# A two-layer float32 kernel on one core: wide and narrow products of a weight tile paired one by one, with a re-laid second norm and modulation products spread earlier

## The chip, the cores and the metric

The kernel runs on one core of one Trainium2 chip. The metric is the device time of one execution in microseconds; the kernel before has a median of 2358.75 us over 3 runs (2356.71 to 2363.08). Its profiled execution took 2357.4 us, of which the trace's span is 2355.7 us. Engine names: PE is the matrix engine (PEld its weight loads), DVE the vector engine, ACT the scalar engine, POOL the general engine, SP the engine that issues most loads.

## The reference

Two blocks follow each other on 256 tokens of width 2048, all in float32. What matters here of the first block:

```
mod = silu(c) @ w_mod + b_mod; sh1, sc1, g1, sh2, sc2, g2 = split(mod, 6)
hx  = rms_norm(x, norm1_g) * (1 + sc1) + sh1
z   = hx @ w_in                       # q, gates, v, g, sb, sc, sh, ga, gb
o   = scan over tokens, both directions, started from the states that ctx leaves
y_a = norm(o) * silu(g);  y_b = sb * short_conv(sc * sh)
x   = x + g1 * ((sigmoid(ga) * (y_a @ w_pa) + sigmoid(gb) * (y_b @ w_pb)) @ w_o)
h   = rms_norm(x, norm2_g) * (1 + sc2) + sh2
a, b = split(h @ w_up, 2);  a = conv 3x3 on a 4 x 64 grid of tokens (a) + bias
x   = x + g2 * ((silu(a) * b) @ w_down)   # 5632 channels
return rms_norm(x, final_g)
```

The second block norms its input with 16 added rows, forms q, k, v and gates by products with `w_in_2`, runs two kinds of attention (one with normed and rotated q and k: `qk_norm`, `diff`; one of a stick-breaking kind: `stick`), and returns the input plus the gated result times `w_out_2`.

## The kernel before

Every large product is done in three float32r parts: each operand is split into a high part and a low rest, and high x high, high x low and low x high are summed in PSUM. Weights come from memory in tiles of 128 x 1024 elements (512 KB), loaded by `blocks`: one load into `raw` on SP's queue, then ACT makes `whi` (L156), then DVE makes `wlo` = raw - whi (L157). There are four buffers each of `raw`, `whi` and `wlo`; 680 tiles go through in all. The two conversions are given a high priority in the ordering of instructions; all other vector work is ordered behind or between them by a list scheduler that sets one fixed order for each engine.

Three forms of product use these tiles. `gemm_tf` (L239 to L241) has the weights as the moving operand, 512 columns each. `gemm_ft` has them as the stationary operand with two sources. `gemm_wide` also has them as the stationary operand: for each 128 x 128 piece of `whi` a product with 512 moving columns (high and low part of the activations beside each other), here called wide, and for each piece of `wlo` a product with 256 columns (the high part alone), here called narrow. Both go through `mat` (L296). A tile holds eight pieces; in the kernel before all eight wide products of a tile come first, then all eight narrow ones. `gemm_wide` is called 32 times (2 in the recurrent stage, 22 in the feed-forward stage, 8 in the second block), 8 tiles each: 256 tiles, 2048 pairs of a wide and a narrow product.

The stages follow each other in time: first norm (0 to 205 us), recurrent (to 430), rest of the mixer (to 1024, its last product is with `w_o`), feed-forward (to 1785; four, four and three steps of `up`, each group followed by `down`), second block (to the end). Work that isn't a large product is written as generators in a list `bg`; `pump`, called after each weight tile, advances them by a step or more. A separate generator, `late_mod`, forms the modulation values that are needed from `w_o` on: in 128 steps it loads 512 KB of `w_mod` on POOL's queue (L663) and multiplies and adds them on DVE (two instructions a step, L697 and L700, of 128 x 512 each). `late_rate` (0.42) is the number of such steps for each pump. Where a value is needed and isn't there yet, the code pumps until it is (`while self.n_mod < 9 + n`).

At the end of the mixer, `add_rows` adds the gated product to x (L1103, L1104), `squares` sums squares on ACT, `rsqrt_mean` makes the factor `r2`, and `ffn` scales x by it on ACT (L1115), turns it by PE (L265) and applies scale and shift (L1125, L1126, L1128). The rows of x were loaded on SP's queue between the last loads of `w_pa` and the loads of `w_o`.

In the feed-forward stage `conv` does the 3 x 3 convolution of an `up` step: 24 instructions on DVE (L1166) and 16 on POOL (L1160, L1162) for 512 channels; it is put into `bg` between the two products of its step. In the second block two DVE multiplications in `qk_norm` (L1515) and `diff` (L1615) read rows that DMAs spread over the partitions; they are pinned, so they stand at a fixed place of DVE's order.

## Time and profile before

| | |
|---|---|
| median of 3 runs | 2358.75 us |
| profiled execution / its span | 2357.4 / 2355.7 us |
| PE busy (share of the span) | 2279.4 us (97%) |
| DVE busy | 1677.1 us (71%) |
| ACT busy | 1103.2 us (47%) |
| POOL busy | 377.0 us (16%) |
| bytes moved | 476.19 MB, mean 202 GB/s |

PE's share is of issued products whose ends are modelled, so it says where PE waits but not how dense its work is. The other columns are averages over stages that differ: DVE is near 60% in some and over 95% in others, and only there can it hold PE up. The granted clock of PE is at its full level (2.4 GHz, shown as 1.00) but for a few short stretches at half of it (1.2 GHz, 0.50).

### The profile page before, as it was taken

The page shows a single profiled execution, that of the slowest core. Times are in us where ns is not written, and L with a number is a line of the kernel's source. Part 1 is how long each engine was busy: PE and PEld are TensorE (multiplying, and loading weights), DVE is VectorE, ACT ScalarE, POOL GpSimd, SP SyncE. Part 2 cuts the span into 40 slices and gives each one's busy share as a digit, 9 for nine tenths or more (in the row PEclk, how much of TensorE's full clock was granted, in tenths as well). Part 3 has the DMA queues.
Part 4 walks back from the last instruction along what each step waited for, and adds up shares of the span by engine and source line. Part 5 has one row for each costly group of instructions (what it writes and reads, how often), then busy time and mean ns, then how long its engine had stood idle before and what let it go on. Part 6 is the DMA issues. An engine that isn't in the chain of part 4 may idle for free. (4 is left out here: it accounts for less than half of the span.)

```text
span 2355.7 us, 33863 instructions
## 1 busy us (share of the span) xinstructions
PE 2279.4 (97%) x12872; PEld 1933.8 (82%) x12872; DVE 1677.1 (71%) x2445; ACT 1103.2 (47%) x1514; POOL 377.0 (16%) x630
## 2 busy tenths in 40 slices
PE   5999999999999999989989999999999999999999
PEld 3689898888888787878777888888888988888887
DVE  3556488788988876888997688757877665653564
ACT  3324344544555543454443445434555463554543
POOL 0200000100001101003540043202220212211000
PEclk9999999999999999999999999999999999999999
DMA  9774443777778778757666666655655657664454
GB/s 317 270 246 158 136 125 120 248 232 240 241 231 269 242 254 315 241 180 232 216 228 214 192 187 184 195 193 186 196 194 183 177 153 162 167 151 126 132 196 155
DMA packets 293123, 476.19 MB, mean 202 GB/s; under 512 B 16153, under 2 KB 151816, under 8 KB 292960
## 3 DMA queue, kind: packets, MB, share of 16 engines
q1 hardware_dynamic: 267120, 387.50, 51.5%
q0 software_dynamic: 25168, 85.50, 12.6%
q8 instruction: 101, 1.65, 0.3%
q10 hardware_dynamic: 672, 1.03, 0.1%
q14 instruction: 62, 0.51, 0.1%
HBM read 468.05 MB, written 2.10 MB: 200 GB/s over the span
## 5 line engine op out<-in xcount | busy, mean ns | idle before, releaser
L156 ACT ACTIVATE whi<-raw 128x1024 fp32r<-128x1024 f32 x680 | 715.7, 1058 | 885.5 <-PE ps L241 399.4
L157 DVE TENSOR_TENSOR wlo<-raw,whi 128x1024 fp32r<-128x1024 f32 x680 | 840.4, 1242 | 364.2 <-ACT whi L156 360.1
L296 PE MATMUL ps<-t,whi 128*128 128x512 f32 (+2 forms) x4096 | 813.4, 343 | 9.1 <-ACT whi L156 5.7
L296 PEld LDWEIGHTS ps<-t,whi 128*128 128x128 f32 x4096 | 633.8, 190 | 108.0 <-issue 26.4
L239 PE MATMUL ps<-whi,t 128*128 128x512 f32 x1376 | 545.3, 396 | 4.2 <-ACT whi L156 4.2
L240 PE MATMUL ps<-wlo,t 128*128 128x512 f32 x1376 | 538.3, 391 | 1.9 <-DVE wlo L157 1.9
L241 PE MATMUL ps<-whi,t 128*128 128x512 f32 x1376 | 538.0, 391 | 0.0
L296 PE MATMUL ps<-t,wlo 128*128 128x256 f32 (+1 forms) x3072 | 441.6, 284 | 18.2 <-DVE wlo L157 18.2
L296 PEld LDWEIGHTS ps<-t,wlo 128*128 128x128 f32 x3072 | 416.2, 190 | 46.6 <-DVE wlo L157 24.1
L239 PEld LDWEIGHTS ps<-whi,t 128*128 128x128 f32 x1376 | 259.4, 189 | 58.8 <-ACT whi L156 4.6
L240 PEld LDWEIGHTS ps<-wlo,t 128*128 128x128 f32 x1376 | 259.5, 189 | 55.3 <-DVE wlo L157 2.7
L241 PEld LDWEIGHTS ps<-whi,t 128*128 128x128 f32 x1376 | 259.3, 188 | 54.2
L663 POOL DMA_DIRECT2D lm<-in_w_mod x128 | 92.8, 725 | 692.7 <-DVE t L697 352.8
L697 DVE SCALAR_TENSOR_TENSOR t<-lm,silc,t 128x512 f32<-128x512 f32 x240 | 180.5, 752 | 5.2 <-DMA lm<-in_w_mod 3.0
L1160 POOL TENSOR_SCALAR cb<-pad,vec 128x256 f32<-128x256 f32 x88 | 84.7, 977 | 430.3 <-DVE pad L211 430.3
L1166 DVE SCALAR_TENSOR_TENSOR t<-pad,vec,t 128x256 f32<-128x256 f32 x264 | 143.6, 573 | 4.3 <-ACT t L1196 2.5
L1162 POOL TENSOR_TENSOR t<-t,cb 128x256 f32<-128x256 f32 x88 | 84.5, 961 | 3.0
L649 DVE TENSOR_TENSOR t<-ps,t 128x256 f32<-128x256 f32 x96 | 36.1, 418 | 57.7 <-PE ps L296 57.6
L296 PE MATMUL ps<-t,t 128*128 128x128 f32 (+5 forms) x352 | 59.1, 332 | 0.8 <-ACT t L1590 0.6
L296 PE MATMUL ps<-em,cstat 128*32 128x512 f32 (+1 forms) x320 | 44.5, 555 | 14.7 <-DVE t L303 11.4
L296 PEld LDWEIGHTS ps<-t,t 128*128 128x128 f32 (+3 forms) x352 | 44.9, 185 | 11.7 <-issue 3.8
L882 ACT ACTIVATE t<-t 128x1024 f32<-128x1024 f32 x28 | 29.6, 1057 | 41.4 <-DVE t L880 36.8
...
## 6 DMA issues: line engine op xcount, KB each, us to landing
...
lm<-in_w_mod POOLq DMA_DIRECT2D x128, 512.0 KB, 5.5
...
```

The source lines that it names most:

```text
L156: a = nc.scalar.activation(out=hi, in_=raw, func=AF.Copy)
L157: b = nc.vector.tensor_tensor(out=lo, in0=raw, in1=hi.bitcast(F32), op=ALU.subtract)
L239: nc.tensor.matmul(b, lhsT=ah(kt + k), rhs=hi[:, k, :], start=first, stop=False)
L240: nc.tensor.matmul(b, lhsT=ah(kt + k), rhs=lo[:, k, :], start=False, stop=False)
L241: nc.tensor.matmul(b, lhsT=al(kt + k), rhs=hi[:, k, :], start=False, stop=last)
L296: self.nc.tensor.matmul(o, lhsT=l, rhs=r, start=start, stop=stop, skip_group_check=True)
L649: nc.vector.tensor_tensor(out=e, in0=o, in1=e, op=ALU.add)
L663: nc.gpsimd.dma_start(out=raw, in_=W[kb * 256:kb * 256 + 256, 2 * D + b * 512:2 * D + b * 512 + 512].rearrange("(k p) f -> p k f", p=128))
L697: nc.vector.scalar_tensor_tensor(out=acc, in0=raw[:, j, :], scalar=s, in1=acc, op0=ALU.mult, op1=ALU.add)
L1160: nc.gpsimd.tensor_scalar(out=cb, in0=tap(j, t), scalar1=wt(t, 4 * n + j), scalar2=1.0, op0=ALU.mult, op1=ALU.mult)
L1162: nc.gpsimd.tensor_tensor(out=a, in0=a, in1=cb, op=ALU.add)
L1166: stt(out=a, in0=tap(j, t), scalar=wt(t, 4 * n + j), in1=a, op0=ALU.mult, op1=ALU.add)
```

## The change

In `gemm_wide` each wide product is followed at once by the narrow one of the same piece. `late_rate` is 0.8 up to the end of the recurrent stage and 0.45 after it. The four loads of x go to POOL's queue, one after each step of the mixer's last loop, whose buffers `mb` are given up on the way. The last `add_rows`, its squares and `rsqrt_mean` are done for one half of the tokens at a time and at high priority; the scaling of x is written ahead of the turning, its first quarter on DVE and ACT, the other three on POOL; and the first product of the feed-forward stage asks for one quarter of its input ahead instead of two. `conv` is put into `bg` behind both products of its step for the first eight steps. The two pinned multiplications of `qk_norm` and of `diff` stand 5 and 8 pump steps apart instead of one.

```diff
--- before.py
+++ after.py
@@ -81,7 +81,7 @@
         self.tc, self.nc, self.I, self.out = tc, nc, I, out
         self.bg = []
         self.late = None
-        self.late_rate = 0.42
+        self.late_rate = 0.8
         self.late_due = 0.0
         self.n_mod = 0
         self.n_name = 0
@@ -187,15 +187,12 @@
         for u in range(0, 4, at_once):
             banks = [self.bank((128, 2, 256)) for _ in range(at_once)]
             for kt, hi, lo in self.blocks(W, r0, nkt, c0 + 128 * u, n=8 // at_once):
-                for w in (hi, lo):
-                    for k in range(8 // at_once):
-                        first, last = kt + k == 0, kt + k == nkt - 1
-                        for j, b in enumerate(banks):
-                            wt = w[:, k, j * 128:(j + 1) * 128]
-                            if w is hi:
-                                self.mat(b, wt, src.both(kt + k), start=first, stop=False)
-                            else:
-                                self.mat(b[:, 0, :], wt, src.hi(kt + k), start=False, stop=last)
+                for k in range(8 // at_once):
+                    first, last = kt + k == 0, kt + k == nkt - 1
+                    for j, b in enumerate(banks):
+                        c = slice(j * 128, (j + 1) * 128)
+                        self.mat(b, hi[:, k, c], src.both(kt + k), start=first, stop=False)
+                        self.mat(b[:, 0, :], lo[:, k, c], src.hi(kt + k), start=False, stop=last)
                 self.pump(n_pump)
             if take is None and o is None:
                 o = self.t4()
@@ -525,9 +522,9 @@
         nc.vector.tensor_tensor(out=B, in0=res[1], in1=col(V_BMOD + k0), op=ALU.add)
         out += [A, B]
 
-    def load_rows(self, ap, i, h):
+    def load_rows(self, ap, i, h, queue=None):
         t = self.t4((128, 1024))
-        self.nc.sync.dma_start(out=t, in_=ap[i * 128:(i + 1) * 128, h * 1024:(h + 1) * 1024])
+        (queue or self.nc.sync).dma_start(out=t, in_=ap[i * 128:(i + 1) * 128, h * 1024:(h + 1) * 1024])
         return t
 
     def norm1(self):
@@ -968,6 +965,7 @@
     def rest(self):
         nc, v = self.nc, self.vec
         W = self.I["w_in"][0]
+        self.late_rate = 0.45
         ax = [self.act(0, i * 128, i * 128 + 128) for i in range(2)]
         tt, stt = nc.vector.tensor_tensor, nc.vector.scalar_tensor_tensor
 
@@ -1059,13 +1057,15 @@
             self.ready.add(y[0].name)
 
         mg = []
+        self.x = [[None, None], [None, None]]
         for n in range(4):
             sg, _ = product(8192 + 512 * n, func=AF.Sigmoid)
             times(self.gemm_tf(self.I["w_pa"][0], 0, 8, 512 * n, aya), sg)
             tt(out=sg, in0=sg, in1=mb[n], op=ALU.add)
+            mb[n] = None
             mg.append(self.hl())
             self.bg.append(merge(sg, mg[-1]))
-        self.x = [[self.load_rows(self.I["x"][0], i, h) for h in range(2)] for i in range(2)]
+            self.x[n % 2][n // 2] = self.load_rows(self.I["x"][0], n % 2, n // 2, nc.gpsimd)
         amg = self.halves(mg)
         while self.n_mod < 8:
             self.pump()
@@ -1080,13 +1080,18 @@
                 self.tc.keep_in_program_order(nc.scalar.preload_act_table_set("natural_log_exp_and_others"))
             while self.n_mod < 9 + n:
                 self.pump()
-            self.add_rows(n, banks, self.gate_rows[0])
-            for i in range(2):
+            if n < 3:
+                self.add_rows(n, banks, self.gate_rows[0])
+                for i in range(2):
+                    self.squares(self.chunk(i, n), ss[:, i, n:n + 1])
+        tot = self.s1((128, 2))
+        self.r2 = self.s1((128, 2))
+        with self.tc.high_priority(offset=AHEAD):
+            for i in range(2):
+                self.add_rows(n, banks, self.gate_rows[0], (i,))
                 self.squares(self.chunk(i, n), ss[:, i, n:n + 1])
-        tot = self.s1((128, 2))
-        nc.vector.tensor_reduce(out=tot, in_=ss, axis=mybir.AxisListType.X, op=ALU.add)
-        self.r2 = self.s1((128, 2))
-        self.rsqrt_mean(self.r2, tot, D, EPS)
+            nc.vector.tensor_reduce(out=tot, in_=ss, axis=mybir.AxisListType.X, op=ALU.add)
+            self.rsqrt_mean(self.r2, tot, D, EPS)
 
     def chunk(self, i, n):
         return self.x[i][n // 2][:, (n % 2) * 512:(n % 2) * 512 + 512]
@@ -1094,13 +1099,13 @@
     def squares(self, x, out):
         self.nc.scalar.activation(out=self.t2(), in_=x, func=AF.Square, accum_out=out)
 
-    def add_rows(self, n, banks, rows):
+    def add_rows(self, n, banks, rows, which=(0, 1)):
 
         nc = self.nc
         r = rows[n // 2][:, (n % 2) * 512:(n % 2) * 512 + 512]
-        for i, b in enumerate(banks):
+        for i in which:
             t, x = self.t2(), self.chunk(i, n)
-            nc.vector.tensor_tensor(out=t, in0=b, in1=r, op=ALU.mult)
+            nc.vector.tensor_tensor(out=t, in0=banks[i], in1=r, op=ALU.mult)
             nc.vector.tensor_tensor(out=x, in0=x, in1=t, op=ALU.add)
 
     def ffn(self):
@@ -1108,12 +1113,24 @@
         stt = nc.vector.scalar_tensor_tensor
         hs = [self.hl() for _ in range(4)]
 
+        scaled = [self.t4((128, 2, 512)) for _ in range(4)]
+        for n, xs in enumerate(scaled):
+            for i in range(2):
+                r = self.r2[:, i:i + 1]
+                if n:
+                    nc.gpsimd.tensor_scalar(out=xs[:, i, :], in0=self.chunk(i, n), scalar1=r, scalar2=1.0,
+                                            op0=ALU.mult, op1=ALU.mult)
+                elif i:
+                    with self.tc.high_priority(offset=AHEAD):
+                        nc.scalar.activation(out=xs[:, i, :], in_=self.chunk(i, n), func=AF.Copy, scale=r)
+                else:
+                    with self.tc.high_priority(offset=AHEAD):
+                        nc.vector.tensor_scalar(out=xs[:, i, :], in0=self.chunk(i, n), scalar1=r, scalar2=None,
+                                                op0=ALU.mult)
+
         def normed():
             for n in range(4):
-                xs = self.t4((128, 2, 512))
-                for i in range(2):
-                    nc.scalar.activation(out=xs[:, i, :], in_=self.chunk(i, n), func=AF.Copy,
-                                         scale=self.r2[:, i:i + 1])
+                xs = scaled[n]
                 hf = self.t4()
 
                 def fn(b, ps):
@@ -1136,7 +1153,7 @@
         n_made = [0]
 
         def wait(k):
-            while n_made[0] < min(4, k // 4 + 2):
+            while n_made[0] < min(4, (k + 2) // 4 + 1):
                 next(made, None)
                 n_made[0] += 1
 
@@ -1199,8 +1216,12 @@
 
             self.gemm_wide(W, 0, 16, 512 * n, ah, take, at_once=2 if n else 4, n_pump=1 + n // 8)
             y, b = self.hl(), []
-            self.bg.append(conv(n, acc, pads, b, y))
+            work = conv(n, acc, pads, b, y)
+            if n >= 8:
+                self.bg.append(work)
             b.append(self.gemm_wide(W, 0, 16, FF + 512 * n, ah, n_pump=2))
+            if n < 8:
+                self.bg.append(work)
             return y
 
         def down(n0, ys, last):
@@ -1514,7 +1535,8 @@
             h = slice(2 * i, 2 * i + 2)
             self.pin(nc.vector.scalar_tensor_tensor(out=x[:, h, :], in0=x[:, h, :], scalar=w, in1=rb[:, h, :],
                                                     op0=ALU.mult, op1=ALU.mult))
-            yield
+            for _ in range(5 - 4 * i):
+                yield
 
         for b in (0, 64):
             nc.gpsimd.dma_start(out=rot[b:b + 8], in_=x[b + 8:b + 16])
@@ -1613,7 +1635,8 @@
         for i in range(2):
             h = slice(2 * i, 2 * i + 2)
             self.pin(nc.vector.tensor_tensor(out=do[:, h, :], in0=do[:, h, :], in1=rb[:, h, :], op=ALU.mult))
-            yield
+            for _ in range(8 - 7 * i):
+                yield
 
 
 _INS = [
```

On PE, in the first product of the first `up` step, whose four PSUM banks are `ps_8998` to `ps_9001`, the rows read as follows before: `t_1526` holds the activations, the last column is partitions x moving columns.

```order
L296 MATMUL ps_8998<-t_1526_8990,whi_9078 128x512
L296 MATMUL ps_8999<-t_1526_8990,whi_9078 128x512
L296 MATMUL ps_9000<-t_1526_8990,whi_9078 128x512
L296 MATMUL ps_9001<-t_1526_8990,whi_9078 128x512
L296 MATMUL ps_8998<-t_1526_8990,wlo_9079 128x256
L296 MATMUL ps_8999<-t_1526_8990,wlo_9079 128x256
L296 MATMUL ps_9000<-t_1526_8990,wlo_9079 128x256
L296 MATMUL ps_9001<-t_1526_8990,wlo_9079 128x256
```

The same tile in the changed kernel, with its own buffer numbers (banks `ps_9092` to `ps_9095`) and line numbers:

```order
L293 MATMUL ps_9092<-t_1549_9072,whi_9143 128x512
L293 MATMUL ps_9092<-t_1549_9072,wlo_9144 128x256
L293 MATMUL ps_9093<-t_1549_9072,whi_9143 128x512
L293 MATMUL ps_9093<-t_1549_9072,wlo_9144 128x256
L293 MATMUL ps_9094<-t_1549_9072,whi_9143 128x512
L293 MATMUL ps_9094<-t_1549_9072,wlo_9144 128x256
L293 MATMUL ps_9095<-t_1549_9072,whi_9143 128x512
L293 MATMUL ps_9095<-t_1549_9072,wlo_9144 128x256
```

Wide products of all four banks followed by narrow ones have become four pairs, each on one bank; what each product multiplies is the same.

On DVE, in the second product of the second `up` step, before: L157 makes `wlo`, L1166 is the convolution, L700 and L697 the modulation products, L211 takes a result out of PSUM.

```order
L700 TENSOR_SCALAR t_1706_10032<-lm_9944,silc 128x512
L1166 SCALAR_TENSOR_TENSOR t_1630_9581<-pad_9798,vec,t_1630_9581 128x256
L697 SCALAR_TENSOR_TENSOR t_1706_10032<-lm_9944,silc,t_1706_10032 128x512
L157 TENSOR_TENSOR wlo_10126<-raw_10123,whi_10125 128x1024
L1166 SCALAR_TENSOR_TENSOR t_1630_9581<-pad_9798,vec,t_1630_9581 128x256
L697 SCALAR_TENSOR_TENSOR t_1706_10032<-lm_10033,silc,t_1706_10032 128x512
L157 TENSOR_TENSOR wlo_10152<-raw_10149,whi_10151 128x1024
```

The same place in the changed kernel (L1183 is the convolution, L208 takes a result out, L253 splits the finished activations, L680 adds a modulation row):

```order
L157 TENSOR_TENSOR wlo_10063<-raw_10060,whi_10062 128x1024
L208 TENSOR_TENSOR t_1706_9980<-ps_9878,t_1706_9980 128x256
L253 TENSOR_TENSOR t_1609_9405<-t_1560_9091,t_1609_9405 128x2x256
L253 TENSOR_TENSOR t_1610_9406<-t_1560_9091,t_1610_9406 128x2x256
L680 TENSOR_TENSOR t_1634_9538<-ps_10009,t_1634_9538 128x512
L157 TENSOR_TENSOR wlo_10092<-raw_10089,whi_10091 128x1024
L1183 SCALAR_TENSOR_TENSOR t_1646_9617<-pad_9861,vec,t_1646_9617 128x256 x2
L157 TENSOR_TENSOR wlo_10140<-raw_10137,whi_10139 128x1024
L157 TENSOR_TENSOR wlo_10164<-raw_10161,whi_10163 128x1024
```

Modulation products and convolution stood between the conversions; now the modulation products are over and the conversions stand closer. Counted over the order, 54 of the 256 modulation products stand behind the second norm before and 18 in the changed kernel; at the end of the recurrent stage 34 are done before and 66 in the changed kernel.

On DVE at the second norm, before: L683 is the last gate row, L1103 and L1104 are `add_rows`, L1087 sums the squares, L303 to L309 are `rsqrt_mean`, L1126 the first modulation of the result.

```order
L683 TENSOR_TENSOR t_1463_8698<-ps_8965,t_1463_8698 128x512
L157 TENSOR_TENSOR wlo_9153<-raw_9150,whi_9152 128x1024
L1103 TENSOR_TENSOR t_1517_8968<-ps_8793,t_1463_8698 128x512
L1103 TENSOR_TENSOR t_1518_8971<-ps_8794,t_1463_8698 128x512
L1104 TENSOR_TENSOR t_1372_8248<-t_1372_8248,t_1517_8968 128x512
L1104 TENSOR_TENSOR t_1374_8252<-t_1374_8252,t_1518_8971 128x512
L1087 TENSOR_REDUCE s_1521_8978<-s_1375_8257 128x2
L303 TENSOR_SCALAR t_1523_8981<-s_1521_8978 128x2
L307 TENSOR_TENSOR t_1524_8982<-s_1522_8980 128x2
L308 SCALAR_TENSOR_TENSOR t_1524_8982<-t_1524_8982,t_1523_8981 128x2
L309 SCALAR_TENSOR_TENSOR s_1522_8980<-t_1524_8982,s_1522_8980 128x2
```

The same place in the changed kernel (L1108, L1109: `add_rows`; L1093: sum of squares; L300 to L306: `rsqrt_mean`; L1128: scaling of the first quarter):

```order
L1108 TENSOR_TENSOR t_1542_9052<-ps_8884,t_1285_7763 128x512
L1109 TENSOR_TENSOR t_1348_8078<-t_1348_8078,t_1542_9052 128x512
L1108 TENSOR_TENSOR t_1544_9057<-ps_8885,t_1285_7763 128x512
L157 TENSOR_TENSOR wlo_9215<-raw_9212,whi_9214 128x1024
L1109 TENSOR_TENSOR t_1400_8345<-t_1400_8345,t_1544_9057 128x512
L1093 TENSOR_REDUCE s_1540_9050<-s_1401_8350 128x2
L300 TENSOR_SCALAR t_1546_9063<-s_1540_9050 128x2
L304 TENSOR_TENSOR t_1547_9064<-s_1541_9051 128x2
L305 SCALAR_TENSOR_TENSOR t_1547_9064<-t_1547_9064,t_1546_9063 128x2
L306 SCALAR_TENSOR_TENSOR s_1541_9051<-t_1547_9064,s_1541_9051 128x2
L1128 TENSOR_SCALAR t_1556_9079<-t_1241_7539,s_1541_9051 128x512
```

The gate row is no longer in the chain, the two halves follow each other, a conversion stands between the last product and the last addition, and a scaling has come to DVE.

## Rows read from the trace of the kernel before

**Rows 1.** Busy time by stretch: stretch, its length, engines, PEclk, DMA share, GB/s.

```profile
300.00:400.00 100.00, 98.95 (x690) 91.74 (x690) 83.73 (x163) 48.36 (x73) 4.63 (x7) 1.00 0.37 111
600.00:700.00 100.00, 99.91 (x490) 84.14 (x489) 93.18 (x148) 57.51 (x68) 9.39 (x13) 1.00 0.74 238
...
1098.00:1125.00 27.00, 25.76 (x148) 22.27 (x146) 24.92 (x34) 18.05 (x26) 6.36 (x6) 1.00 0.69 215
1125.00:1150.00 25.00, 21.01 (x114) 16.74 (x112) 23.48 (x34) 5.39 (x8) 17.04 (x29) 1.00 0.72 236
1150.00:1200.00 50.00, 44.04 (x232) 36.74 (x233) 45.86 (x62) 22.46 (x31) 22.05 (x35) 0.97 0.68 223
1200.00:1245.00 45.00, 39.91 (x214) 33.24 (x213) 44.93 (x63) 20.21 (x27) 17.01 (x20) 0.97 0.69 224
```

**Rows 2.** Modulation products (L697) alone, early feed-forward: DVE busy, PEclk, DMA, GB/s.

```profile
1098.00:1245.00 147.00, 28.97 (x37) 0.98 0.69 224
```

**Rows 3.** Busy time in stretches around a lowered clock; columns as in group 1.

```profile
935.90:941.80 5.90, 5.38 (x12) 3.76 (x12) 4.49 (x5) 2.03 (x2) 0.00 (x0) 0.50 0.98 363
...
1187.50:1190.90 3.40, 3.40 (x12) 2.74 (x11) 2.00 (x4) 0.00 (x0) 3.40 (x17) 0.51 0.88 264
1242.10:1245.60 3.50, 3.38 (x8) 2.70 (x9) 3.50 (x7) 0.00 (x0) 0.00 (x0) 0.51 1.00 377
```

**Rows 4.** Timeline, start of `w_o`: start, length, what, idle before it.

```profile
912.69 2.15 SPq L530 DMA_DIRECT2D t<-in_x  x4
...
934.84 1.06 ACT L156 ACTIVATE whi<-raw 128x1024 fp32r<-128x1024 f32 x1 [13.28 <-DMA raw<-in_w_o]
...
935.95 0.79 PE L239 MATMUL ps<-whi,t 128*128 128x512 f32 x1 [4.18 <-ACT whi L156]
```

**Rows 5.** Timeline, second norm, from the last product of `w_o` on.

```profile
1022.75 0.40 PE L241 MATMUL ps<-whi,t 128*128 128x512 f32 x1
...
1024.04 0.69 DVE L683 TENSOR_TENSOR t<-ps,t 128x512 f32<-128x512 f32 x1 [1.27 <-PE ps L296]
1024.65 1.22 DVE L157 TENSOR_TENSOR wlo<-raw,whi 128x1024 fp32r<-128x1024 f32 x1
1025.78 1.28 DVE L1103 TENSOR_TENSOR t<-ps,t 128x512 f32<-128x512 f32 x2
1026.98 1.28 DVE L1104 TENSOR_TENSOR t<-t,t 128x512 f32<-128x512 f32 x2
...
1030.40 1.33 ACT L1115 ACTIVATE t<-t,s 128x512 f32<-128x512 f32 x2 [0.62 <-DVE s L309]
...
1031.18 2.15 PE L265 MATMUL ps<-cst,t 128*128 128x128 f32 x8 [7.18 <-ACT t L1115]
...
1034.94 2.06 PE L296 MATMUL ps<-t,whi 128*128 128x512 f32 x4
```

**Rows 6.** The page's groups by line: busy, mean ns, idle before.

```profile
L296 PEld LDWEIGHTS ps<-t,wlo 128*128 128x128 f32 x3072 | 416.2, 190 | 46.6 <-DVE wlo L157 24.1
...
L1160 POOL TENSOR_SCALAR cb<-pad,vec 128x256 f32<-128x256 f32 x88 | 84.7, 977 | 430.3 <-DVE pad L211 430.3
```

**Rows 7.** Timeline of PE: products of 512 columns, then one steady tile of `gemm_wide`.

```profile
1012.32 0.39 PE L240 MATMUL ps<-wlo,t 128*128 128x512 f32 x1
...
1013.45 0.39 PE L239 MATMUL ps<-whi,t 128*128 128x512 f32 x1
...
1351.16 2.00 PE L296 MATMUL ps<-t,whi 128*128 128x512 f32 x8
1353.01 1.12 PE L296 MATMUL ps<-t,wlo 128*128 128x256 f32 x8
1353.96 0.63 PE L296 MATMUL ps<-t,whi 128*128 128x512 f32 x2
```

**Rows 8.** Timeline, second block: a pinned multiplication and the product behind it.

```profile
1961.38 0.69 DVE L1615 TENSOR_TENSOR t<-t,t 128x512 f32<-128x512 f32 x1 [6.30 <-DMA t<-t]
...
1963.26 0.52 PE L296 MATMUL ps<-t,wlo 128*128 128x272 f32 x2 [2.42 <-DVE wlo L157]
```

## The prediction

> **What bounds the kernel now.** First the page's busy shares: PE is busy for nearly the whole span, so a gain must come from stretches where PE waits, from those where its clock is halved, or from denser products. The busy times by stretch show where it waits. Between 1098 and 1245 us DVE is busy 139.2 of 147 us and PE idle 1.24 + 3.99 + 5.96 + 5.09 = 16.3 us [rows 1]; elsewhere DVE at 93% does not hold PE up (600 to 700 us, PE idle 0.1 us) [rows 1]. In that stretch 29 us of DVE's time are late modulation products [rows 2]. Three short stretches at half of PE's clock, 1.2 GHz, lie behind waits [rows 3]. The timeline then names two single waits: PE stands 4.18 us at the start of `w_o` because ACT waited 13.28 us for a weight load that was issued behind four loads of x [rows 4], and from 1024.0 to 1031.2 us through the chain of the second norm [rows 5]. So the kernel is bound by PE's product rate, plus some 40 us of such losses.
>
> The sum is made against the profiled execution, 2357.4 us, of which 2355.7 us are the span and 1.7 us lie around it; the median of the runs, 2358.75 us, is 1.35 us more, and the forecast is put on that median.
>
> **Early feed-forward stage: fewer modulation products in DVE's way.** By the order, 36 of the 54 modulation products behind the second norm go to earlier places. 37 of the 54 lie between 1098 and 1245 us and take 28.97 us there, 0.78 us each [rows 2]. So 17 lie before this stretch, and with 18 left in all about one stays in it: DVE needs 139 - 28 = 111 us where PE, without its waits and slow clock, needs 147 - 16.3 - 3.4 = 127 us. If the rest is put behind the same work as before, 7 of the 18 stay in the stretch, and it is 116 us: 91% at most, below the 93% of the stretch of 600 to 700 us, which has no waits. What goes: the 16.3 us of idle time, and two stretches of half clock, 3.4 and 3.5 us long [rows 3], half of each lost, 3.4 us; 19.7 us in all. Bounds: nothing, if other work keeps DVE full, and -19.7. I take -17.5, near the upper end, since the stretch just before 1098 us keeps the 18 products and will still be tight. The convolutions are now written behind both products of their step, but in the order the last one of the first four still ends some 15 DVE instructions before the first `add_rows` of `down`, as before: no new wait there.
>
> **Start of `w_o`.** The four x loads leave SP's queue and go to POOL's, one in each step of the loop before. What goes: PE's 4.18 us and the half clock of 935.9 to 941.8 us, in which PE was busy 5.38 us, so some 2.7 us lost [rows 3, 4]: 6.9 us. The DMA engines were full there (share 0.98, 363 GB/s) [rows 3]. The Trainium skill (Trainium Kernel Development and Optimization, Key Constraints) says that loads from SP, ACT and POOL queues share the same 16 engines, and that another queue saves only issue time; by that the change of queue alone is worth nothing, and the wait would stay: a rival below. What helps by the rows is the time: three of the four loads come some 20 to 100 us sooner, and only the last competes with `w_o`. If it takes its quarter of the wait, 1.7 us stay; bounds -6.9 and -5.2, I take -6. On POOL's queue the modulation loads stand behind the x loads; by the order 212 modulation products are done at `w_o`'s start where its first addition needs 152, so nobody waits for those.
>
> **Second norm.** Before, counted from the start of the last product plus its 0.4 us (1023.15 us): first turning after 8.0 us, first product after 11.8 us [rows 5]. In the changed order the gate row (0.69 us) is gone and the chain is: two additions of the first half, the product of the second half, one conversion, the last addition, at 1.28 / 2 = 0.64 us each and 1.22 us for the conversion [rows 5]: 0.64 x 4 + 1.22 = 3.8 us. From the last addition (1026.98 + 1.28) to the start of scaling took 2.14 us [rows 5]; scaling one half (1.33 / 2) 0.67 us: first turning after 6.6 us. Eight turnings stand together and took 2.15 us [rows 5], so the first product comes after about 8.7 us: -3.1 us. The three quarters that POOL scales are hidden: no row shows it at 128 x 512; the nearest, 128 x 256, takes 977 ns [rows 6], so six take 5.9 us (same price) to 11.7 us (twice), and the second quarter (two of them) is needed a tile pair, 5.6 us, behind the first product. The first wide products there take 2.06 / 4 = 0.52 us each [rows 5], over twice the 0.23 of a steady one: the clock is down behind this wait too, and a shorter wait may end that sooner. Bounds -1.4 (the turning alone) and -5; I take -3.
>
> **Pairs.** 2048 pairs, and PE has nothing to hide them under, so each ns of a pair is 2.05 us. In a steady tile eight wide products take 1353.01 - 1351.16 = 1.85 us, 231 ns each, and eight narrow ones 0.95 us, 119 ns each [rows 7]: 350 ns a pair. Products of 512 columns that follow each other take (1013.45 - 1012.32) / 5 = 226 ns [rows 7]; so wide ones pay some 5 ns for having narrow ones near. No row shows strict alternation. Lower end: 226 + 119 = 345 ns, -10 us. Upper end: a weight load takes 190 ns [rows 6] and a narrow product 119; if the next wide one had to wait for all of it, 71 ns a pair, +145 us. Against that end: the narrow run itself has such a load before each product and still goes at 119 ns [rows 6, 7], and the wide run behind it starts on time (1353.96) [rows 7]. I take the value of the near rows with a little of the 5 ns back: -2 ns, -4 us. The Trainium skill (TensorE: Matmul & The Clock Gate, LDWEIGHTS) puts a weight load of 128 columns at about 107 ns, as long as 256 columns of work, and (Part 2, step 1) lets it run under the product before; by that rule a load fits under a narrow product in either order and the term would be 0, the sum -25 instead of -29. The measured 119 ns of a load and its narrow product agree with such a load that is hidden, not with one that is added.
>
> In pairs the first narrow product needs its `wlo` some 1.6 us sooner, and a `whi` buffer comes free at the tile's end instead of 0.95 us before it. A late `wlo` now holds the seven wide products behind it in PE's order, and ACT's next conversion waits for them. Of PE's waits for `wlo` most lie in the stretch relieved above; two or three longer ones in the second block are in `gemm_ft`, which keeps its order. Bounds 0 and +9 (some five waits by 1.8 us); I take +2.
>
> **Elsewhere.** In the recurrent stage 32 more modulation products run, 32 x 0.78 = 25 us, where DVE is busy 84 of 100 us [rows 1]. They share what room is left; bounds 0 and +25, I take +1.5, because 93% did no harm [rows 1]. In the second block the second pinned multiplication waited 6.30 us for its DMA right behind the first and held a conversion and PE 2.42 us [rows 8]; eight pumps later its data will be there: -2.4 at best, 0 if the first wait alone suffices. I take -2.
>
> **Sum:** -17.5 - 6 - 3 - 4 + 2 + 1.5 - 2 = -29 us. 2357.4 - 29 = 2328.4 us for a profiled execution; 2358.75 - 29 = 2330 us for the median.
>
> **Rivals.**
> - Slower: the weight load shows. Place: each wide product of the 256 tiles, behind a narrow one too short to cover a load. At the full 71 ns +145 us replace the -4, so 2330 + 149 = 2479 us. It decides from 29 - 4 = 25 us, 12 ns a pair; at 30 ns, 2330 + 4 + 61 = 2395 us. For: 190 ns against 119 [rows 6]. Against: the narrow runs. 5%.
> - Alternation is as dense as a pure run of either kind, or denser: 345 ns or a little less, -10 to -20 us in place of -4: 2314 to 2324 us. For: the 5 ns that the wide run pays. 15%.
> - Alternation keeps the extra cost at each change: +3 to +6 ns a pair are +6 to +12 us in place of the -4: 2340 to 2346 us. For: the extra comes where the width changes. 15%.
> - The early modulation products choke the stage they go to: DVE at 84 + 11 of 100 us between 300 and 400 us [rows 1]; if none of the 25 us is hidden, 2330 + 23 = 2353 us. Against: 93% elsewhere. 8%.
> - The shared DMA engines: the x loads collide with weights at another place and the `w_o` wait stays: 2330 + 6 = 2336 us. 6%.
> - The change doesn't do what it says for DVE, because the freed room fills with convolutions: 5 of the 17.5 us come: 2342 us. For: DVE has work waiting throughout. 6%.
> - No change to speak of: several of these at once, 2352 to 2366 us. 4%.
> My own case holds the rest, 41%; its range is 2322 to 2338 us.
>
> About 0.3%, 7 us, is what a measurement of this kernel can tell from no change. Faster takes all but the slower case, the no-change case and half of the choked stage: 0.87; same 0.08; slower 0.05. The range reaches over the dense case to 2310 us and over the cost at each change and the DVE case to 2346 us; the choked stage, no change and slower (17%) lie outside.
>
> **What would show it.** In the changed profile: one steady pair in `gemm_wide` at 345 to 350 ns from wide to wide; DVE under 93% and PE idle under 4 us in the stretch of the first four `up` steps; no wait of ACT for `w_o` loads over 5 us; from the last `w_o` product to the first wide product under 10 us; DVE's second wait at the pinned multiplication gone. A pair over 356 ns, or waits for `wlo` in the recurrent stage, would make the prediction wrong.

## The result and the profile after

The changed kernel takes 2333.71 us (median of 4 runs, 2331.9 to 2338.03) against 2359.03 us of the kernel before (4 runs, 2356.71 to 2363.08): 25.3 us faster, ratio 0.9893 with a 95% interval of 0.9873 to 0.9914. The forecast was 2330 us, range 2310 to 2346. The time lies in the range, but not every part does: two of them were wrong in opposite directions, and this section and the experiments show which. One run of the experiments (2502.82 us, with the convolution back between the products) was in a slower state at a lower clock and is left out of its median.

First the busy shares and the group of the products with `wlo` through `mat` on the page of the changed kernel (busy us, share, instructions; then busy, mean ns):

```profile
PE 2277.8 (98%) x12872; PEld 1934.4 (83%) x12872; DVE 1684.0 (72%) x2446; ACT 1103.6 (47%) x1509; POOL 377.7 (16%) x640
...
L293 PE MATMUL ps<-t,wlo 128*128 128x256 f32 (+1 forms) x3072 | 733.8, 284 | 6.3 <-DVE wlo L157 6.3
```

PE's busy time is that of before (2279.4 us). It can't show denser or looser products, since a matmul's end is modelled; the starts do. Then the busy times by stretch (columns as in [rows 1]):

```profile
300.00:400.00 100.00, 97.90 (x678) 90.52 (x677) 91.48 (x174) 46.65 (x72) 8.71 (x13) 1.00 0.47 147
600.00:700.00 100.00, 100.00 (x489) 84.50 (x488) 94.97 (x154) 58.15 (x69) 10.11 (x14) 1.00 0.75 240
...
935.00:945.00 10.00, 10.00 (x49) 8.29 (x49) 3.13 (x3) 3.83 (x5) 0.72 (x1) 1.00 1.04 387
...
1030.00:1098.00 68.00, 63.93 (x357) 55.28 (x356) 57.43 (x89) 31.53 (x45) 23.71 (x49) 0.96 0.64 209
1098.00:1245.00 147.00, 145.11 (x788) 123.55 (x787) 131.52 (x173) 75.19 (x99) 45.27 (x78) 1.00 0.60 189
```

Between 1098 and 1245 us PE is idle 147 - 145.11 = 1.9 us, where [rows 1] had 16.3; at the start of `w_o` it is busy throughout at the full clock, where [rows 3, 4] had a wait of 4.18 us and the half clock. The third stretch to look at is the one ahead, 1030 to 1098 us: PE is idle 4.1 us there and its clock is at 0.96. In the kernel before PE had no idle time there once the wait of the second norm was over:

```profile
1060.00:1098.00 38.00, 38.00 (x219) 33.16 (x217) 33.58 (x49) 15.42 (x23) 23.13 (x37) 1.00 0.71 235
```

The second norm, from the last product of `w_o` on (answers to [rows 5]):

```profile
1018.29 0.39 PE L238 MATMUL ps<-whi,t 128*128 128x512 f32 x1
...
1024.18 4.49 POOL L1121 TENSOR_SCALAR t<-t,s 128x512 f32<-128x512 f32 x6 [82.49 <-DVE s L306]
1024.65 1.99 PE L262 MATMUL ps<-cst,t 128*128 128x128 f32 x8 [5.97 <-DVE t L1128]
...
1027.59 0.76 PE L293 MATMUL ps<-t,whi 128*128 128x512 f32 x1 [0.95 <-DVE t L1145]
```

From the last product's end (1018.68 us) the first turning comes after 6.0 us and the first wide product after 8.9 us; 6.6 and 8.7 were forecast, 8.0 and 11.8 were those of before. POOL scales 128 x 512 elements in 4.49 / 6 = 0.75 us, below the 0.98 us taken as the lower price. The half clock behind the wait did not get shorter: the granted clock is at 0.50 for 10.2 us in both kernels, from 1027.1 to 1037.3 us before and from 1021.5 to 1031.7 us now.

One steady tile (eight pairs and the start of the next tile, to hold against [rows 7]):

```profile
1329.89 0.40 PE L293 MATMUL ps<-t,whi 128*128 128x512 f32 x1
1330.12 0.28 PE L293 MATMUL ps<-t,wlo 128*128 128x256 f32 x1
1330.24 0.40 PE L293 MATMUL ps<-t,whi 128*128 128x512 f32 x1
...
1332.72 0.40 PE L293 MATMUL ps<-t,whi 128*128 128x512 f32 x1
```

Eight pairs take 1332.72 - 1329.89 = 2.83 us, 354 ns a pair: the wide product's successor starts 0.23 to 0.24 us later, the narrow one's 0.12. Before it was 1.85 + 0.95 = 2.80 us. So alternation is looser than runs, not denser.

Where did the time go? Since both kernels issue the same 11,296 large products, the start of the n-th one in one trace can be set against the n-th in the other. The difference (changed minus before) at the end of each stretch:

| stretch of the kernel before | difference at its end | change in it |
|---|---|---|
| start to 36 us | -0.4 us | |
| first norm, recurrent, rest of the mixer (to 903 us) | +3.4 | +3.8 |
| start and course of `w_o` (to 986) | -4.5 | -7.9 |
| second norm (to 1035) | -7.4 | -2.9 |
| first `up` steps (to 1095) | -0.2 | +7.2 |
| next ones (to 1303) | -21.2 | -21.0 |
| rest of the feed-forward stage (to 1756) | -17.5 | +3.7 |
| second block | -22.6 | -5.1 |

The +7.2 us was not forecast. The timeline of its end shows the larger part of it (POOL's convolution and the issue of a load behind it, DVE, PE):

```profile
1058.94 2.23 POOL L1177 TENSOR_SCALAR cb<-pad,vec 128x256 f32<-128x256 f32 x2 [25.82 <-DVE pad L208]
...
1070.91 1.21 DVE L157 TENSOR_TENSOR wlo<-raw,whi 128x1024 fp32r<-128x1024 f32 x1
...
1076.07 0.76 POOL L660 DMA_DIRECT2D lm<-in_w_mod  x1
...
1080.49 0.75 DVE L694 SCALAR_TENSOR_TENSOR t<-lm,silc,t 128x512 f32<-128x512 f32 x1 [6.50 <-DMA lm<-in_w_mod]
...
1082.43 0.39 PE L293 MATMUL ps<-t,wlo 128*128 128x256 f32 x1 [3.63 <-DVE wlo L157]
```

DVE stands 6.50 us for a modulation load. POOL issues that load at 1076.07 us, after 17 us of convolution that began at 1058.94 us. Behind DVE's wait stands a conversion, and PE waits 3.63 us for it; a half clock of 3.4 us follows, 1.7 us lost: 5.3 of the 7.2 us. An estimated 0.9 us more are the half clock behind the second norm, of which 4.1 us are left at the first wide product and 2.4 were before; the remaining 1 us is not traced. The Trainium skill (PSUM — Partial Sum Buffer, Engine vs sequencer instructions) says that the queues of ACT, DVE and POOL are strictly first in, first out; the rows agree, for the load came late although DMA had room (a share of 0.50 from 1058.94 to 1076.07 us).

### The profile page after: what moved, and what is told of

It is laid out like the page before. It is cut to its first block, busy times and chain, and to the rows that moved or that the text cites. A ratio compares the mean times of both kernels' runs of the same rounds, so it can differ in the third digit from the quotient of the medians.

```text
span 2333.4 us, 33893 instructions
## 1 busy us (share of the span) xinstructions
PE 2277.8 (98%) x12872; PEld 1934.4 (83%) x12872; DVE 1684.0 (72%) x2446; ACT 1103.6 (47%) x1509; POOL 377.7 (16%) x640
## 3 DMA queue, kind: packets, MB, share of 16 engines
q8 instruction: 101, 1.65, 0.3%
## 4 chain that ended last, share of the span: by engine, by line
PE 86%; DVE 4%; DMA 4%; issue 3%; POOL 1%; ACT 1%; SPq 0%; POOLq 0%; DVEq 0%; ACTq 0%
PE ps L293 44%; PE ps L236 13%; PE ps L238 13%; PE ps L237 13%; DMA t<-t 1%; DVE wlo L157 1%; DMA raw<-in_w_in 1%; PE ps L262 1%; ACT whi L156 1%; DVE t L1183 1%; DMA lm<-in_w_mod 0%; DMA em<-in_w_mod 0%; SPq L492 0%; POOL t L1179 0%; POOL cb L1177 0%
## 5 line engine op out<-in xcount | busy, mean ns | idle before, releaser
L157 DVE TENSOR_TENSOR wlo<-raw,whi 128x1024 fp32r<-128x1024 f32 x680 | 847.4, 1251 | 362.4 <-ACT whi L156 358.2
L293 PE MATMUL ps<-t,whi 128*128 128x512 f32 (+2 forms) x4096 | 1021.9, 346 | 7.5 <-ACT whi L156 2.5
L293 PEld LDWEIGHTS ps<-t,whi 128*128 128x128 f32 x4096 | 651.9, 190 | 129.4 <-issue 25.4
L293 PE MATMUL ps<-t,wlo 128*128 128x256 f32 (+1 forms) x3072 | 733.8, 284 | 6.3 <-DVE wlo L157 6.3
L293 PEld LDWEIGHTS ps<-t,wlo 128*128 128x128 f32 x3072 | 528.2, 191 | 12.3 <-DVE wlo L157 8.6
L1183 DVE SCALAR_TENSOR_TENSOR t<-pad,vec,t 128x256 f32<-128x256 f32 x264 | 141.2, 571 | 1.3
L1179 POOL TENSOR_TENSOR t<-t,cb 128x256 f32<-128x256 f32 x88 | 78.7, 895 | 1.1
L207 ACT ACTIVATE t<-ps 128x256 f32<-128x256 f32 x84 | 31.1, 374 | 44.5 <-PE ps L293 44.3
```

The lines of the kernel that those rows point to most:

```text
L157: b = nc.vector.tensor_tensor(out=lo, in0=raw, in1=hi.bitcast(F32), op=ALU.subtract)
L293: self.nc.tensor.matmul(o, lhsT=l, rhs=r, start=start, stop=stop, skip_group_check=True)
L1179: nc.gpsimd.tensor_tensor(out=a, in0=a, in1=cb, op=ALU.add)
L1183: stt(out=a, in0=tap(j, t), scalar=wt(t, 4 * n + j), in1=a, op0=ALU.mult, op1=ALU.add)
```

## The experiments

Each time is a median, and each difference to the kernel before is against its runs on the same chip in between.

**The pairs alone, and the pairs taken back.** The first is the kernel before with the new loop, the second the changed kernel with the old one:

```diff
-                for w in (hi, lo):            # all eight wide, then all eight narrow
-                    for k in range(8 // at_once):
-                        ...
+                for k in range(8 // at_once):
+                    ...
+                        self.mat(b, hi[:, k, c], src.both(kt + k), start=first, stop=False)
+                        self.mat(b[:, 0, :], lo[:, k, c], src.hi(kt + k), start=False, stop=last)
```

Expected of the first: 

> The kernel before with the pairs alone. Theory A (alternation itself costs PE some 4 ns a pair: in the changed kernel's steady tiles a wide product is followed 237 ns later by its narrow one and that 118 ns later by the next wide one, 354 ns, against 350 ns in the runs of before): 2048 x 4 = 8 us slower, 2367 us, and 354 ns a pair in every steady tile. Theory B (the pairs are free, the spacing in the changed kernel comes from other work beside them): 2359 us, 350 ns. Theory C (pairs also bring waits for wlo, which is needed 1.6 us sooner): over 2372 us, with more PE waits for wlo between 1098 and 1245 us than the 16.3 us of before.

Expected of the second: 

> The changed kernel with eight wide, then eight narrow products a tile, as before. Theory A (alternation costs 4 ns a pair): 8 us faster than the changed kernel, 2326 us, 350 ns a pair. Theory B (the pairs are free): 2334 us. Theory C (the pairs save waits or clock elsewhere that the runs bring back): slower than the changed kernel, 2338 us or more.

The first took 2366.57 against 2357.95 us: 8.6 us slower, ratio 1.0034 (1.0022 to 1.0047). The second took 2320.57 us, 13.1 us faster than the changed kernel: ratio to the kernel before 0.9842 (0.9828 to 0.9855), clear of the changed kernel's 0.9873 to 0.9914. Eight pairs of the first take 2.83 us, as in the changed kernel (from 1350.15 to 1352.98 us). A steady tile of the second and the start of the next:

```profile
1330.38 2.00 PE L296 MATMUL ps<-t,whi 128*128 128x512 f32 x8
...
1333.17 2.00 PE L296 MATMUL ps<-t,whi 128*128 128x512 f32 x8
```

2.83 us in pairs, 2.79 in runs, whatever stands beside them: theory A holds for the spacing, and theory B falls. In the second block the spacing costs nothing that can be seen (the median tile is 2.81 us in pairs and 2.82 in runs), so it explains at most about 5 of the 13.1 us: that is what the runs gain by the n-th large product up to the end of the feed-forward stage. The other 9.2 of the traces' 14.3 us come in the second block. With the pairs alone, too, only about half of the loss in the trace lies ahead of the second block (some 4 us, and some 4 in it), so it is partly luck that 8.6 us meet theory A's 8. PE's waits there, in the changed kernel, and the stretch in both (first the changed kernel's):

```profile
PE ps L293 <- ACT t L1612: 3.3, 2, 2.4
PE ps L293 <- DVE t L1265: 1.5, 1, 1.5
PE ps L293 <- DVE t L1299: 1.5, 1, 1.5
```

```profile
1770.00:2215.00 445.00, 436.41 (x2926) 387.12 (x2925) 259.40 (x365) 223.88 (x362) 71.60 (x123) 0.99 0.60 155
...
2195.00:2210.00 15.00, 14.33 (x59) 10.69 (x59) 5.90 (x8) 7.93 (x18) 1.44 (x2) 0.77 0.18 56
```

```profile
1765.00:2201.00 436.00, 433.04 (x2925) 384.73 (x2924) 259.32 (x366) 224.74 (x362) 70.52 (x123) 1.00 0.61 159
```

PE is idle 8.6 us in pairs and 3.0 us in runs, and in pairs a half clock of 6.8 us near 2200 us is added: 5.6 + 3.4 = 9.0 us. So waits are there as well, as theory C of the first run has them, but most of them are not for `wlo`, as it said: PE stands at small products of the attention. The longest one, in the changed kernel and then in runs (ACT's conversion ahead of it, PE):

```profile
2051.40 1.04 ACT L156 ACTIVATE whi<-raw 128x1024 fp32r<-128x1024 f32 x1
...
2052.86 1.33 PE L293 MATMUL ps<-t,t 128*128 128x256 f32 x5 [2.44 <-ACT t L1612]
```

```profile
2042.45 1.87 PE L296 MATMUL ps<-t,t 128*128 128x256 f32 x8 [0.43 <-ACT t L1615]
```

PE's own order is the same in both kernels at this place. ACT's order is not: in pairs two exponentials and then the weight conversion stand ahead of the copy (L1612) that PE waits for, in runs the conversion comes first and one exponential. Why the scheduler ordered it so was not tried; a `whi` buffer that comes free later in pairs would fit, but that is not shown.

**Half runs.** The changed kernel with four wide, four narrow, and so on:

```diff
+                for h in range(2):
+                    for w in (hi, lo):
+                        for k in range(h * 4 // at_once, (h + 1) * 4 // at_once):
```

Expected: 

> The changed kernel with four wide, four narrow, four wide, four narrow products a tile. In the runs of before the wide products at places 1 to 5 behind a narrow run are 233, 236, 228, 232 and 231 ns apart and the rest 227 ns. Theory D (a wide product pays while it is near the narrow ones, whatever the run's length): the four wide ones of each run cost 232 ns each on the mean, 352 ns a pair, 4 us faster than the changed kernel, 2330 us. Theory E (each change from narrow to wide costs a fixed time, (354 - 350) x 8 / 7 = 4.6 ns): one change more than in runs of eight, 1.2 us over them, 2327 us, and 350.6 ns a pair.

It took 2325.62 us, between runs and pairs; two half runs:

```profile
1329.77 1.09 PE L297 MATMUL ps<-t,whi 128*128 128x512 f32 x4
1330.70 0.64 PE L297 MATMUL ps<-t,wlo 128*128 128x256 f32 x4
...
1332.58 1.09 PE L297 MATMUL ps<-t,whi 128*128 128x512 f32 x4
```

A tile takes 1332.58 - 1329.77 = 2.81 us, 351 ns a pair. Neither theory holds: a second change a tile costs some 14 ns, three times the 4.6 of theory E, and 351 is below the 352 of theory D. What is shown is that the tile gets longer with more changes, though not in proportion: 2.79, 2.81, 2.83 us for one, two and eight. What inside PE costs that time stays open.

**Modulation loads on SP's queue.** The changed kernel with the loads of the last 16 steps moved:

```diff
-            nc.gpsimd.dma_start(
+            (nc.sync if b >= 14 else nc.gpsimd).dma_start(
                 out=raw, in_=W[kb * 256:kb * 256 + 256, ...
```

Expected: 

> The changed kernel with the loads of the last 16 modulation steps on SP's queue; the orders of PE, DVE and ACT are the same. Theory A (DVE's wait of 6.50 us at 1074 to 1080.5 us comes from the modulation load that POOL issues only behind its 17 us of convolution, and it costs PE 3.63 us of waiting and half of 3.4 us of half clock): the wait goes, 5.4 us faster than the changed kernel, 2328 us. Theory B (DVE has too much to do there anyway and PE waits a little later): 2332 to 2335 us, PE's idle time between 1078 and 1150 us stays near 5 us. Theory C (on SP's queue the modulation loads hold up the weight loads behind them): 2336 us or more, with ACT waiting for loads of up.

It took 2333.2 us, no change (the changed kernel: 2333.71). Theory B's time, but not for B's reason. The load came in time, and then:

```profile
1074.57 0.61 POOL L286 DMA_DIRECT2D t<-in_b_mod  x1
...
1081.17 0.69 DVE L680 TENSOR_TENSOR t<-ps,t 128x512 f32<-128x512 f32 x1 [5.32 <-DMA t<-in_b_mod]
```

The bias row of the last gate stands in the same queue behind the same convolution, and DVE waits for it in place of the load; behind it PE waits 4.1 us.

**Both on SP's queue, with runs.** The same with the bias row moved too, and with eight wide, then eight narrow:

```diff
-                    self.gate_rows[b // 8].append(self.row(self.I["b_mod"][0], 2 * D + 512 * b, 1024))
+                    self.gate_rows[b // 8].append(self.row(self.I["b_mod"][0], 2 * D + 512 * b, 1024,
+                                                               nc.sync if b >= 14 else None))
```

Expected: 

> The changed kernel with eight wide, then eight narrow products again, and with the last 16 modulation loads and the last gate's bias row on SP's queue. Theory A (the wait near 1080 us is POOL's queue: behind the convolution stood first the modulation load, then the bias row; with both moved it is gone): 5 us faster than the runs alone, 2315.5 us, no PE wait over 1.5 us between 1075 and 1095 us. Theory B (the wait turns up at a third place): 2319 to 2322 us with 3 us or more of PE waiting between 1075 and 1100 us.

It took 2314.06 us, 6.5 us under the 2320.57 of runs alone; ratio to the kernel before 0.9812 (0.9799 to 0.9826, just clear of the 0.9828 to 0.9855 of runs alone). The stretch of the wait:

```profile
1075.00:1095.00 20.00, 20.00 (x116) 17.57 (x115) 19.93 (x34) 7.46 (x10) 0.00 (x0) 1.00 0.81 265
```

PE is busy throughout and at the full clock: the wait was POOL's queue. DVE works 19.93 of 20 us and holds nobody up.

**The loads of x, on POOL's and on SP's queue.** The kernel before with the loads in the mixer's last loop:

```diff
             tt(out=sg, in0=sg, in1=mb[n], op=ALU.add)
+            mb[n] = None
             ...
-        self.x = [[self.load_rows(self.I["x"][0], i, h) for h in range(2)] for i in range(2)]
+            self.x[n % 2][n // 2] = self.load_rows(self.I["x"][0], n % 2, n // 2, nc.gpsimd)  # or nc.sync
```

Expected on POOL's queue: 

> The kernel before with the four x loads alone moved: one on POOL's queue after each step of the mixer's last loop. Theory A (ACT's wait of 13.28 us goes, and with it PE's 4.18 us and the half clock of 935 to 942 us): 6 to 9 us faster than before, 2350 us; no PE wait over 1 us at the start of w_o. Theory B (the loads only collide with other weights): under 3 us, 2355 us or more, with ACT still waiting over 5 us for a load of w_o.

Expected on SP's queue: 

> The kernel before with the four x loads at the same earlier places, but on SP's queue between the weight loads; the orders of PE and ACT are those of the kernel with POOL's queue. Theory A (the time of the loads decides, not their queue): within 2 us of the kernel with POOL's queue, 2350 us. Theory B (the queue decides, since a weight load stands behind each x load): 3 us or more slower than that one, with ACT waiting for weights of w_pa and w_in between 840 and 935 us.

POOL's queue: 2351.25 against 2358.36 us, 7.1 us faster (0.9956 to 0.9981). SP's queue: 2353.57 us, 4.8 us faster (0.9968 to 0.9989). The start of `w_o` with POOL's queue, then with SP's:

```profile
935.00:945.00 10.00, 10.00 (x47) 8.28 (x46) 5.94 (x7) 5.43 (x7) 0.72 (x1) 1.00 0.99 364
```

```profile
935.00:945.00 10.00, 9.24 (x43) 7.05 (x41) 2.83 (x3) 3.20 (x4) 0.72 (x1) 1.00 1.03 385
```

Both lose the long wait and the half clock, though the DMA engines are as full as before; SP's queue leaves a wait of 0.76 us for `wlo`. The time of the loads does most of it. Whether the queue adds the other 2.3 us the overlapping intervals don't settle.

**The rates alone.** The kernel before with `late_rate` 0.8, then 0.45.

```diff
-        self.late_rate = 0.42
+        self.late_rate = 0.8
     def rest(self):
+        self.late_rate = 0.45
```

Expected: 

> The kernel before with the modulation rate of 0.8, then 0.45 alone (the convolution stays between the two products). Theory A (DVE's time in the early feed-forward stage is what PE waits for there): PE's 16.3 us of waiting between 1098 and 1245 us and the half clock go but for some 5 us, the recurrent stage gets some 4 us longer, 11 us faster in all, 2347 us. Theory B (the room fills with convolution): PE still waits 10 us or more there, 2354 us or more.

It took 2341.11 against 2358.36 us, 17.3 us faster (ratio 0.9919 to 0.9944). Its stretches:

```profile
300.00:400.00 100.00, 97.99 (x680) 90.53 (x679) 90.88 (x173) 46.53 (x72) 9.20 (x13) 1.00 0.48 146
...
1098.00:1245.00 147.00, 142.67 (x777) 122.89 (x778) 129.86 (x176) 75.26 (x101) 47.04 (x78) 0.99 0.60 189
```

By the n-th large product the stretch of 1095 to 1312 us gives 18.5 us back and the stages up to 855 us take 4.1 us, 2.7 of them the recurrent one: theory A, with more gain than its 11 us.

**The second norm alone.** The kernel before with the new `add_rows`, `scaled` and `wait`, as the diff of the change shows them.

Expected: 

> The kernel before with the second norm's part alone: last addition by halves and at high priority, scaling ahead of the turning (DVE, ACT, POOL), one quarter asked for ahead. Theory A (the chain got shorter by itself): from the last w_o product's end to the first turning 6.0 us in place of 8.0 with the gate row out of the chain, or 7 us if the gate row is still in it; to the first wide product 9 us in place of 11.8; 3 us faster, 2355 us. Theory B (most of the gain came with the rate, which took the gate row out of the chain: in the kernel with the rates alone PE's wait there fell from 7.18 to 6.08 us): under 1.5 us faster, 2357 us.

It took 2358.78 against 2357.6 us, no change (0.9992 to 1.001). The gate row and the first turning in it, and then the same turning in the kernel with the rates alone:

```profile
1023.24 0.69 DVE L683 TENSOR_TENSOR t<-ps,t 128x512 f32<-128x512 f32 x1 [1.27 <-PE ps L296]
...
1030.39 1.99 PE L265 MATMUL ps<-cst,t 128*128 128x128 f32 x8 [7.19 <-DVE t L1128]
```

```profile
1032.31 2.15 PE L265 MATMUL ps<-cst,t 128*128 128x128 f32 x8 [6.08 <-ACT t L1116]
```

With the gate row still in the chain PE waits 7.19 us, as in [rows 5]; with the rates alone, which take the row out, 6.08. By the n-th large product the rates alone gain 2.0 us between 1023 and 1035 us, and the changed kernel 2.9: theory B.

**The pins alone.** The kernel before with the two pinned multiplications 5 and 8 pump steps apart.

```diff
-            yield
+            for _ in range(5 - 4 * i):   # in diff: 8 - 7 * i
+                yield
```

Expected: 

> The kernel before with the two pinned multiplications of each kind 5 and 8 pump steps apart, alone. Theory A (DVE no longer stands behind the second transfer): PE's waits near 1961 us (2.42 us) and 2015 us (3.35 us) and the half clock behind them shrink, 2 to 4 us faster, 2355 us. Theory B (the first multiplication's wait decides): within 1 us of before, with the same waits.

It took 2344.89 against 2357.6 us, 12.7 us faster (0.9931 to 0.9956): three to six times what theory A gave. Three of PE's other waits in the second block of the kernel before, beside the 2.42 us of [rows 8]:

```profile
1987.51 1.21 PE L296 MATMUL ps<-t,wlo 128*128 128x256 f32 x8 [0.66 <-DVE wlo L157]
2018.77 1.28 PE L296 MATMUL ps<-t,wlo 128*128 128x272 f32 x8 [3.35 <-DVE wlo L157]
...
2031.62 1.09 PE L1403 MATMUL ps<-cst,t 128*128 128x128 f32 x8 [1.65 <-DVE t L1346]
```

and the stretch in the kernel before and with the pins apart:

```profile
1785.00:2238.00 453.00, 440.80 (x2941) 389.29 (x2940) 263.02 (x371) 223.98 (x364) 73.23 (x123) 1.00 0.59 155
```

```profile
1786.00:2225.00 439.00, 435.98 (x2939) 387.21 (x2938) 262.17 (x371) 226.60 (x365) 70.38 (x123) 1.00 0.61 160
```

PE is idle 12.2 us before and 3.0 us now. A half clock of 3.4 us at 2201 us is gone too, 1.7 us; the rest of the 12.7 us is not accounted for. (The half clock that the expectation puts behind the waits near 1961 and 2015 us is not in the trace of the kernel before: the granted clock is 1.00 there.) DVE's waits for the pinned rows are not gone. They fall from 51.9 to 36.9 us, up to 6.5 us at a first multiplication and 3.95 us at a second one, but PE no longer waits for a `wlo` behind them. In the changed kernel, at the place of [rows 8] (the second multiplication, then PE):

```profile
1953.50 0.69 DVE L1637 TENSOR_TENSOR t<-t,t 128x512 f32<-128x512 f32 x1 [5.36 <-DMA t<-t]
...
1957.25 0.39 PE L293 MATMUL ps<-t,wlo 128*128 128x256 f32 x1 [0.75 <-DVE wlo L157]
```

So eight pump steps did not bring the second transfer in time there; the wait of PE behind it is 0.75 us in place of 2.42.

**The convolution back between the products.** The changed kernel with runs, and with `conv` put into `bg` where it was.

```diff
-            if n >= 8:
-                self.bg.append(work)
+            self.bg.append(conv(n, acc, pads, b, y))
             b.append(self.gemm_wide(W, 0, 16, FF + 512 * n, ah, n_pump=2))
```

Expected: 

> The changed kernel with eight wide, then eight narrow products again, and with the convolution written between the two products of its step as before. Theory A (putting the convolution behind both products brought the wait near 1083 us; the kernel with the rates alone, which keeps the old place, has none): the wait goes and nothing else comes, 5 us faster than the runs alone, 2315.5 us. Theory B (the new place also relieved DVE: with the old one PE waits as in the kernel with the rates alone, 0.79 + 1.61 + 0.64 + 2.03 us and half of 3.4 us of half clock between 1097 and 1187 us): the two cancel, 2319 to 2322 us, with the waits at other times. Theory C (POOL's queue holds the loads up at either place): 2320 us or more and a wait over 3 us near 1083 us.

It took 2321.6 us (median of four) against the 2320.57 of runs alone (0.9833 to 0.986 against 0.9828 to 0.9855): no difference to be told. Its stretches, then those of runs alone:

```profile
1075.00:1095.00 20.00, 19.27 (x110) 16.43 (x109) 16.79 (x29) 5.86 (x7) 4.75 (x16) 1.00 0.84 273
1098.00:1200.00 102.00, 97.49 (x542) 83.92 (x541) 93.73 (x132) 52.56 (x74) 31.68 (x56) 0.98 0.62 189
```

```profile
1075.00:1095.00 20.00, 16.76 (x89) 14.46 (x88) 12.72 (x20) 5.66 (x7) 4.71 (x16) 0.91 0.74 236
1098.00:1200.00 102.00, 100.15 (x566) 86.76 (x566) 95.58 (x131) 53.73 (x72) 33.02 (x56) 1.00 0.64 194
```

Theory B: with the old place PE is idle 0.7 and 4.5 us in the two stretches, with the new one 3.2 and 1.9, and either has one short half clock. So the shifted convolution brought the wait at POOL's queue and took away others of the same size.

**Gentler rates.** The fastest kernel with 0.6 and 0.5 in place of 0.8 and 0.45.

Expected: 

> The fastest kernel so far (runs again, last modulation loads and bias row on SP's queue) with rates 0.6 and 0.5 in place of 0.8 and 0.45. Theory A (the 4 us that the recurrent stage lost grow with the modulation products put there): a quarter of the products goes to the next stage, which has room, 1 to 2 us faster, 2312.5 us. Theory B (the next stage, with DVE at 95% busy between 600 and 700 us, is full): 2314 us or more, with PE waits between 430 and 1000 us that were not there.

2312.47 us, ratio 0.9807 (0.9793 to 0.982): 1.6 us under the 2314.06, but the intervals overlap. By the n-th large product, against the fastest kernel, the recurrent stage is 2.2 us shorter up to 317 us, and most of the gain is given back by 1000 us. One stretch of that:

```profile
600.00:700.00 100.00, 99.47 (x486) 83.26 (x485) 95.82 (x153) 56.55 (x67) 11.55 (x16) 1.00 0.75 246
```

PE is idle 0.53 us, where the fastest kernel, like the changed one, had none: theory B's mechanism. Of the 2.7 us between the two traces 1.6 lie in the second block, where the profiled execution at the higher rates had a half clock near 2181 us; whether the rates have to do with that is not shown.

## Why the prediction was right, and where it was not

That the total came so near is luck: two errors of opposite sign nearly cancel. The pairs with their waits were put at -2 us and cost 8.6 to 13.1; the pins were put at -2 and gain 12.7 alone. The parts, forecast, alone and in the changed kernel:

| part | forecast | alone | in the changed kernel |
|---|---|---|---|
| rates (both stages) | -17.5 + 1.5 | -17.3 | +3.8 early, -13.8 from 1035 to 1303 us, pairs and the new wait included |
| x loads | -6 | -7.1 | -7.9 |
| second norm | -3 | +1.2 (no change) | -2.9 |
| pairs, with their waits | -4 + 2 | +8.6 | -13.1 when taken back |
| pins | -2 | -12.7 | in the second block's -5.1 |
| convolution | 0 | | no difference when taken back, in the kernel with runs |

- **Early feed-forward stage: right, in mechanism and size.** DVE's modulation products held PE up, 18.5 us came back with the rates alone, and PE's idle time in that stretch is 1.9 us. The step "no new wait there" failed: it looked at DVE's order for the convolution and not at POOL's queue, in which the modulation loads and a bias row stand behind the convolution. That cost 5.3 of the 7.2 us up to 1095 us; with both loads on SP's queue it is gone.
- **Recurrent stage: the mechanism right, the size low.** 1.5 us were taken; the stage itself takes 3.7 us more in the changed kernel and 2.7 with the rates alone, and all stages up to `w_o` 3.8 and 4.1, inside the bounds of 0 to 25. "93% did no harm" does not carry over to this stage: at 91% DVE, PE is idle 2.1 of 100 us, where it was 1.05 before, and its waits there are for results of ACT and DVE that small products need.
- **Start of `w_o`: right.** Nothing of the wait stayed, where 1.7 us were left to the last load; the 7.1 us alone lie just beyond the bound of 6.9. By the Trainium skill (Trainium Kernel Development and Optimization, Key Constraints), which says that all queues share the 16 engines, the move of queue alone was worth nothing; the run on SP's queue, 4.8 of the 7.1 us, agrees that the earlier time does most of it.
- **Second norm: the size right, the cause half wrong.** The chain ended as forecast (8.9 us to the first product, 8.7 forecast). But the gate row, counted here, left the chain through the rates, and the norm's own edits are worth nothing while it is there (2358.78 against 2357.6 us). The hope that a shorter wait ends the half clock sooner did not come true: 10.2 us in both kernels.
- **Pairs: wrong in sign.** The step that failed is "I take the value of the near rows with a little of the 5 ns back: -2 ns". The row of a wide run showed that products near narrow ones cost more, and with eight changes a tile instead of one there was more of that, not less. The rival that keeps the extra cost at each change had it: +3 to +6 ns a pair, measured +4 to +5 (354 against 349 to 350 ns). The slower rival, 12 ns and more, falls. The Trainium skill's price (TensorE: Matmul & The Clock Gate, LDWEIGHTS), by which a load is hidden in either order and the term is 0, is nearer than the -4 taken, but no run here gives 0.
- **Waits for `wlo` in pairs: wrong kind.** Of the 6.3 us that PE waits for `wlo` in the changed kernel 3.6 are POOL's queue. What came were waits for small products in the second block, 5.6 us, and 3.4 us of lost clock, shown by taking the pairs back. With the pairs alone the second block costs only some 4 us in the trace; beside the pins' change it costs 9.2, and why it is more there is not shown.
- **Pins: right in sign, half right in mechanism, six times too small.** The step "eight pumps later its data will be there" failed at the very place it was read from: DVE still waits 5.36 us there in the changed kernel and 3.95 with the pins alone. What the distance changed is what stands behind that wait: PE waits 0.75 us and 0 there in place of 2.42. And the sum priced one wait. In the kernel before PE also waited 0.66 us behind another second multiplication, 3.35 us behind a first one (DVE 7.55 us for its transfer), 1.65 us behind a pinned multiplication by other rows (L1530, DVE 3.35 us), and 1.16 us at 2100.76 us for a conversion that ACT made only after a further second one. Why the waits behind first multiplications went as well was not tried.
- **The signs.** Of those listed, DVE under 93% and PE idle under 4 us in the early feed-forward stage, no wait of ACT for `w_o` over 5 us (the longest is 3.0) and under 10 us at the second norm came. A pair at 345 to 350 ns (354) and the second pinned wait gone did not. Neither sign of being wrong came: no pair over 356 ns, no wait of PE for `wlo` in the recurrent stage.

The parts run alone sum to 8.6 - 17.3 - 7.1 + 1.2 - 12.7 = -27.3 us; measured are -25.3. That is near, but they do not simply add: the pairs alone cost 8.6 us and 13.1 among the rest, and no part run alone shows the wait at POOL's queue. The version that the runs point to (all of the change but the pairs, with the last modulation loads and bias row on SP's queue) beats both kernels: 2314.06 us, 44.3 us under the kernel before.
